# A 512-column product over both halves of the activations, and an earlier first up load, in a float32 transformer chain

## The chip, the core and the metric

The kernel runs on one core of one Trainium2 chip. The metric is the device time of the whole kernel in microseconds (us). Five engines work side by side: TensorE (PE) multiplies, its weight loads are listed as PEld; VectorE (DVE) and ScalarE (ACT) work element by element; GpSimd (POOL) does little here; SyncE (SP) issues the weight loads. Each engine takes its own instructions in a fixed order and waits on semaphores for the others.

## The reference, cut to what matters

Two models run one after the other; the change touches the first, `first_block`, alone. It has two layers, and in each layer two feed-forward networks of the same form, so four of them run in all.

```python
def swiglu(h, w_in, w_out):              # h 256 x 1024, w_in 1024 x 5632, w_out 2816 x 1024
    gate, up = jnp.split(h @ w_in, 2, axis=-1)
    return (jax.nn.silu(gate) * up) @ w_out

for l in range(DEPTH):                   # DEPTH = 2
    x = x + 0.5 * swiglu(rms_norm(x, ffn1_norm[l]), ffn1_w_in[l], ffn1_w_out[l])
    x = x + hybrid_mixer(rms_norm(x, mix_norm[l]), ...)
    x = x + 0.5 * swiglu(rms_norm(x, ffn2_norm[l]), ffn2_w_in[l], ffn2_w_out[l])
```

The second model (attention, a long convolution, a dense feed-forward network and a mixture of eight experts) follows and is left as it is.

## The kernel before, in words

**Two parts of each number.** Every float32 operand is split into a high part, which a fast product takes exactly, and the low rest. `split` does that: ACT copies the high part (L251), DVE subtracts it from the source (L252). A product of two such operands is then three products on PE, made by `mm3`: high by high (L290), high by low (L291), low by high (L292).

**Weights.** Weights are loaded 1 MB at a time by `load_raw` (L258) into one of three raw buffers (`wr_66`, `wr_67`, `B_72`) that are used in turn; SP issues these loads in one order. `cut` splits a raw buffer, 1024 columns at a time, into pair buffers (`wp_68` to `wp_71`, `B_73`, `B_74`), which are also used in turn. So the high copy waits until the load has landed and until PE has done with the weights that the pair buffer held before.

**The feed-forward network.** `ffn` walks over the 2816 inner columns in units of 512 (five full units and one of 256). A unit is up (two loads, `w_in`), the next unit's gate (two loads, `w_in`) and down (two loads, `w_out`). The first unit's gate and up are made the other way round, with the activations as PE's weights, and aren't touched by the change beyond the load. For every later unit the inner `gemm` makes a group of 128 inner columns by all 256 tokens with `gemm_feat`: 8 steps over the 1024 inputs, three products of 256 columns in each, 24 products in all, and two groups share one bank of PSUM. `Silu` (ACT, L414) or the multiplication of up by gate (DVE, L433) reads that bank whole, 512 columns at once.

**Banks.** `mmb` hands out the two banks of PSUM named `mm` in turn. PE may begin a new bank only when what was in it has been read.

**Activations.** `feat` lays out the split activations. For 1024 inputs by 256 tokens it makes one tile of high parts and one tile of low parts (`t_77`, `t_78`).

**Order.** A scheduler places the instructions of all engines when the program is built. Background work of the second model (its modulation vectors, L852 to L879, and its long filters, L949 to L1025) is strewn over these stages at low priority.

Of the kernel before, what the change touches and what calls it, by code (L numbers as in the profile page):

```python
# [20 lines left out]
P = 128  # L21
D = 1024
KD = D // P
S = 256
NB = S // P
DFF = 2816
# [91 lines left out]
class Feat:  # L118
# [3 lines left out]

    def span(self, k, n, s):
        c = slice(k % self.per, k % self.per + n)
        hi, lo = self.parts[k // self.per]
        return hi[:, c, s], lo[:, c, s]

    def at(self, k, s):
        hi, lo = self.parts[k // self.per]
        return hi[:, k % self.per, s], lo[:, k % self.per, s]  # L130


class Entry:
# [38 lines left out]
class K:  # L172
# [64 lines left out]
        return self.sb.tile([P, 2048], dt, tag=tag, name=self.nm(tag), bufs=self.BUFS[tag])  # L237

    def feat(self, kt, T):
        per = min(kt, 2048 // T)  # L240
        parts = []
        for _ in range(0, kt, per):
            if per * T <= 1024:
                t = self.tile([P, 2, per, T], "feat", dt=F32R)
                parts.append((t[:, 0], t[:, 1]))
            else:
                parts.append(tuple(self.tile([P, per, T], "feat", dt=F32R) for _ in range(2)))
        return Feat(parts, per)

    def split(self, hi, lo, src, eng=None):  # L250
# [51 lines left out]
    def gemm_feat(self, out, hT, wk, c0, s=slice(0, S)):  # L302
        kt = len(wk)
        c = slice(c0, c0 + P)
        for k in range(kt):
            wh, wl = wk[k]
            self.mm3(out, wh[:, c], wl[:, c], *hT.at(k, s), k == 0, k == kt - 1)

    def tok_steps(self, out, hT, b, wk):
        s = slice(b * P, (b + 1) * P)  # L310
# [67 lines left out]
    def ffn(self, jobs, nb=NB):  # L378
        nc = self.nc
        units = []  # L380
        for job in jobs:
            F = job["w"][0].shape[1]
            for f0 in range(0, F, 512):
                n = min(512, F - f0)
                units.append((job, f0, n, f0 + n == F))

        def gemm(hT, wk, n):
            if nb == 1:
                pg = self.mmb()[:, :n]
                self.gemm_tok(pg, hT, 0, wk)  # L390
                yield pg
                return
            T = nb * P
            for c0 in range(0, n, 2 * P):
                pg = self.mmb()
                for c in range(2):
                    self.gemm_feat(pg[:, c * T : (c + 1) * T], hT, wk, c0 + c * P)
                yield pg

        def gate(job, f0, n, last):  # L400
            if f0 == 0:
# [14 lines left out]
            return out  # L416

        def up(job, f0, n, last, parts):
            wk = job.pop("up", None) or self.load_wk(job["w"][1], f0, n)
            out = []  # L420
            if f0 == 0 and nb > 1:
                out = [self.tile([P, 2, 512], "gT", dt=F32R) for _ in range(n // S)]
# [64 lines left out]
        for i, u in enumerate(units):  # L487
            parts = up(*u, nxt)
# [13 lines left out]
            else:  # L502
                tail(*u[:3], held, parts, u[0]["next"]())

    def ffn_first(self, x, entry, w_in, w_out, nxt):
        nc = self.nc

        def end(b, dn):
            for h in range(2):
                c = slice(h * 512, (h + 1) * 512)  # L510
                nc.vector.scalar_tensor_tensor(
                    out=x[:, b, c], in0=dn[h], scalar=0.5, in1=x[:, b, c], op0=ALU.mult, op1=ALU.add
                )

        got = []

        def after():
            got.append(nxt and Entry(self, x, *nxt))
            return got[0]

        self.ffn([dict(w=(w_in[:, :DFF], w_in[:, DFF:], w_out), hT=entry.hT, first=entry.gemm(), end=end, next=after)])
        return got[0]

    def conv_glu(self, hT, w):
# [1209 lines left out]
def body(k, outs):  # L1734
# [13 lines left out]
    k.nr, k.nw = -1, -1  # L1748
    e.fetch()
    e.fetch()  # L1750
    load(1)
    e.rows(1)

# [4 lines left out]
        k.plan_filters()  # L1758
    for l in range(2):
        k.quota = QUOTAS[2 * l]  # L1760
        e = k.ffn_first(x, e, A["ffn1_w_in"][l], A["ffn1_w_out"][l], mix[l])
        e = k.mixer(x, l, e, ins["ffn2"][l])
        if l == 1:
            hT = k.feat(KD, 4 * P)
            k.plan_ctx(hT)
        k.quota = QUOTAS[2 * l + 1]
        e = k.ffn_first(x, e, A["ffn2_w_in"][l], A["ffn2_w_out"][l], None if l else ins["ffn1"][1])
# [50 lines left out]
```

## Time and profile before

| what | value |
|---|---|
| median of 3 runs | 2943.09 us (2939.08 to 2945.89) |
| profiled execution, its own time | 2937.49 us |
| span of its trace | 2935.8 us |
| PE busy | 2850.5 us (97%) |
| DVE busy | 2201.8 us (75%) |
| ACT busy | 1588.2 us (54%) |
| mean granted TensorE clock | 0.991 |

The profiled execution is one run, 5.6 us below the median of the timed runs. The span is the time from its first to its last instruction, 1.7 us less than its own time. Busy times are means over stages that are unlike each other; a stage has to be looked at by itself.

### The profile page before, as it was taken

How to read it: one execution, taken by the hardware profiler on the slowest of the kernel's cores; microseconds unless marked ns; L12 is line 12 of the kernel's file. 1: busy time of each engine (PE TensorE's matmuls, PEld its weight loads, DVE VectorE, ACT ScalarE, POOL GpSimd, SP SyncE). 2: the span in 40 equal slices, each digit the busy share in tenths (PEclk: the TensorE clock that was granted, in tenths of full speed). 3: DMA queues.
4: the chain of work that ended last, by engine and by line, in shares of the span. 5: the costliest groups of instructions: out<-in, count | busy, mean ns of one | idle time of the engine just before them, and what ended most of it. 6: DMA issues, size and time to landing. Idle time of an engine off the chain costs nothing. (4 is left out here: it accounts for less than half of the span.)

```text
span 2935.8 us, 40815 instructions
## 1 busy us (share of the span) xinstructions
PE 2850.5 (97%) x15778; PEld 2449.8 (83%) x15778; DVE 2201.8 (75%) x3391; ACT 1588.2 (54%) x2365; POOL 169.0 (6%) x249
## 2 busy tenths in 40 slices
PE   7999999999999998999999999999899999999997
PEld 6998789899878997888788888788788888888886
DVE  6778677777977756654458876666698999999997
ACT  5545654554475554432343323544487777777775
POOL 1000200100010000000000000100000000000000
PEclk9999999999999999999999999999999999999999
DMA  7654466656546643142334653335799999999995
GB/s 257 221 197 168 145 217 225 215 202 225 200 140 213 212 155 120 58 111 100 129 126 162 201 201 113 100 106 157 258 347 340 331 358 345 348 350 348 345 339 188
DMA packets 286922, 629.19 MB, mean 214 GB/s; under 512 B 12318, under 2 KB 59152, under 8 KB 286592
## 3 DMA queue, kind: packets, MB, share of 16 engines
q1 hardware_dynamic: 260160, 552.11, 54.0%
q0 software_dynamic: 26128, 73.93, 7.8%
q8 instruction: 126, 2.06, 0.3%
q14 instruction: 76, 0.62, 0.1%
q10 hardware_dynamic: 432, 0.46, 0.0%
HBM read 622.70 MB, written 3.75 MB: 213 GB/s over the span
## 5 line engine op out<-in xcount | busy, mean ns | idle before, releaser
L252 DVE TENSOR_TENSOR wp<-wr,wp 128x1024 fp32r<-128x1024 f32 (+3 forms) x449 | 528.0, 1189 | 167.8 <-ACT wp L251 161.4
L251 ACT ACTIVATE wp<-wr 128x1024 fp32r<-128x1024 f32 (+3 forms) x449 | 453.6, 1030 | 303.9 <-PE mm L292 83.0
L290 PE MATMUL mm<-t,wp 128*128 128x256 f32 (+1 forms) x1360 | 449.7, 331 | 0.4 <-ACT t L414 0.2
L292 PE MATMUL mm<-t,wp 128*128 128x256 f32 (+1 forms) x1360 | 425.4, 314 | 0.2 <-DVE wp L252 0.2
L291 PE MATMUL mm<-t,wp 128*128 128x256 f32 (+1 forms) x1360 | 424.5, 312 | 0.0
L252 DVE TENSOR_TENSOR B<-B,B 128x1024 fp32r<-128x1024 f32 x302 | 361.5, 1222 | 53.6 <-ACT B L251 50.9
L251 ACT ACTIVATE B<-B 128x1024 fp32r<-128x1024 f32 x302 | 312.8, 1055 | 121.1 <-PE acc L292 37.2
L290 PE MATMUL mm<-wp,t 128*128 128x512 f32 (+2 forms) x880 | 343.2, 392 | 5.7 <-ACT t L251 2.5
L291 PE MATMUL mm<-wp,t 128*128 128x512 f32 (+2 forms) x880 | 340.4, 387 | 4.2 <-DVE wp L252 4.1
L292 PE MATMUL mm<-wp,t 128*128 128x512 f32 (+2 forms) x880 | 339.2, 387 | 4.0 <-DVE t L252 4.0
L291 PE MATMUL acc<-wp,t 128*128 128x512 f32 (+2 forms) x760 | 289.8, 383 | 2.5 <-DVE wp L252 2.4
L290 PE MATMUL acc<-wp,t 128*128 128x512 f32 (+2 forms) x760 | 284.9, 386 | 4.3 <-ACT t L251 3.2
L292 PE MATMUL acc<-wp,t 128*128 128x512 f32 (+2 forms) x760 | 285.5, 383 | 1.4 <-DVE t L252 1.3
L290 PEld LDWEIGHTS mm<-t,wp 128*128 128x128 f32 x1360 | 259.6, 191 | 20.7 <-issue 8.2
L291 PEld LDWEIGHTS mm<-t,wp 128*128 128x128 f32 x1360 | 259.9, 191 | 19.1 <-issue 8.7
L252 DVE TENSOR_TENSOR wp<-B,wp 128x1024 fp32r<-128x1024 f32 x208 | 247.5, 1220 | 36.8 <-ACT wp L251 35.4
L292 PEld LDWEIGHTS mm<-t,wp 128*128 128x128 f32 x1360 | 259.1, 191 | 15.8 <-issue 1.0
L251 ACT ACTIVATE wp<-B 128x1024 fp32r<-128x1024 f32 x208 | 215.7, 1056 | 70.6 <-PE mm L292 37.2
L861 DVE SCALAR_TENSOR_TENSOR B<-B,cs,B 128x256 f32<-128x256 f32 x560 | 250.6, 480 | 3.7
L290 PEld LDWEIGHTS mm<-wp,t 128*128 128x128 f32 x880 | 167.5, 190 | 39.3 <-ACT t L251 4.4
L292 PEld LDWEIGHTS mm<-wp,t 128*128 128x128 f32 x880 | 167.4, 190 | 36.9 <-DVE t L252 6.1
L291 PEld LDWEIGHTS mm<-wp,t 128*128 128x128 f32 x880 | 167.5, 190 | 36.1 <-DVE wp L252 6.6
(378 smaller groups left out, 5388.0 us busy)
## 6 DMA issues: line engine op xcount, KB each, us to landing
B<-in_moe_w_gate_dram SPq DMA_DIRECT2D x65, 1024.0 KB, 7.2
B<-in_moe_w_up_dram SPq DMA_DIRECT2D x63, 1024.0 KB, 7.1
B<-in_moe_w_down_dram SPq DMA_DIRECT2D x62, 1024.0 KB, 6.8
wr<-in_ffn_w_in_dram SPq DMA_DIRECT2D x60, 1024.0 KB, 5.2
B<-in_w_mod_dram POOLq DMA_DIRECT2D x48, 1024.0 KB, 5.9
B<-in_ffn_w_in_dram SPq DMA_DIRECT2D x28, 1024.0 KB, 5.1
wr<-in_ffn_w_out_dram SPq DMA_DIRECT2D x28, 1024.0 KB, 4.9
wr<-in_w_in_dram SPq DMA_DIRECT2D x28, 1024.0 KB, 5.2
```

The costliest lines, as they stand in the source:

```text
L251: self.nc.scalar.activation(hi, src, AF.Copy)
L252: (eng or self.nc.vector).tensor_tensor(out=lo, in0=src, in1=hi.bitcast(F32), op=ALU.subtract)
L290: mm(out, lhsT=lh, rhs=rh, start=first, stop=False)
L291: mm(out, lhsT=lh, rhs=rl, start=False, stop=False)
L292: mm(out, lhsT=ll, rhs=rh, start=False, stop=last)
L861: nc.vector.scalar_tensor_tensor(out=acc, in0=raw[:, kk], scalar=cs[:, v, kk : kk + 1], in1=acc, op0=ALU.mult, op1=ALU.add)
```

## The change

In every feed-forward network of the first block, all units but the first: the high weights take the high and the low part of the activations as one moving operand of 512 columns (`gemm_two`), and the low weights take the high part alone into the second half of the same bank. A group of 128 inner columns now fills a bank by itself, with 8 products of 512 columns and 8 of 256. The two halves have to be added: ACT copies the second half into a new tile `sums`, DVE adds the first half, and `Silu` and the multiplication read `sums`. So that a step's high and low parts lie in one tile, `feat` makes two tiles of four steps each, with both parts in each. Apart from that, the first load of the first network's up weights is written directly behind the two loads of the gate, and `up` takes it over as `begun`.

```diff
     def feat(self, kt, T):
-        per = min(kt, 2048 // T)
+        per = min(kt, (1024 if T == S else 2048) // T)
         parts = []
         for _ in range(0, kt, per):
             if per * T <= 1024:
                 t = self.tile([P, 2, per, T], "feat", dt=F32R)
-                parts.append((t[:, 0], t[:, 1]))
+                parts.append((t[:, 0], t[:, 1], t))
...
+    def both(self, k):
+        return self.parts[k // self.per][2][:, :, k % self.per]
...
+    def gemm_two(self, out, hT, wk, c0):
+        mm = self.nc.tensor.matmul
+        c = slice(c0, c0 + P)
+        kw = dict(skip_group_check=True)
+        for k in range(len(wk)):
+            wh, wl = wk[k]
+            x = hT.both(k)
+            mm(out, lhsT=wh[:, c], rhs=x, start=k == 0, stop=k == len(wk) - 1, **kw)
+            mm(out[:, S:], lhsT=wl[:, c], rhs=x[:, 0], start=False, stop=k == len(wk) - 1, **kw)
...
             for c0 in range(0, n, 2 * P):
-                pg = self.mmb()
+                sums = self.tile([P, 512], "sums")
                 for c in range(2):
-                    self.gemm_feat(pg[:, c * T : (c + 1) * T], hT, wk, c0 + c * P)
-                yield pg
+                    pg = self.mmb()
+                    self.gemm_two(pg, hT, wk, c0 + c * P)
+                    part = sums[:, c * S : (c + 1) * S]
+                    nc.scalar.activation(part, pg[:, S:], AF.Copy)
+                    nc.vector.tensor_tensor(out=part, in0=part, in1=pg[:, :S], op=ALU.add)
+                yield sums
...
         def up(job, f0, n, last, parts):
-            wk = job.pop("up", None) or self.load_wk(job["w"][1], f0, n)
+            begun = job.pop("begun", None)
+            if begun:
+                rest = job["w"][1].rearrange("(k p) n -> p k n", p=P)[:, 4:, f0 : f0 + n]
+                wk = self.cut(*begun) + self.load_w(rest)
+            else:
+                wk = job.pop("up", None) or self.load_wk(job["w"][1], f0, n)
...
     e.fetch()
     e.fetch()
+    up = k.load_raw(A["ffn1_w_in"][0].rearrange("(k p) n -> p k n", p=P)[:, :4, DFF : DFF + 512])
     load(1)
```

The scheduler's order differs from before in the four feed-forward stages and the stretches that border on them (there in background work and its loads), and in a branch at the end of the program (a second pass over the experts, for more than 128 tokens of one expert); elsewhere it is the same. At three places it shows what moves.

**On PE, the second unit's gate.** `mm_846` and `mm_807` are a bank of PSUM, `wp` and `B` weights, `t_77` and `t_78` activations. Before, two steps over the inputs and the start of the third:

```order
L290 MATMUL mm_846<-t_77,wp_70 128x256 [waits DVE_49]
L291 MATMUL mm_846<-t_78,wp_70 128x256
L292 MATMUL mm_846<-t_77,wp_70 128x256
L290 MATMUL mm_846<-t_77,wp_70 128x256
L291 MATMUL mm_846<-t_78,wp_70 128x256
L292 MATMUL mm_846<-t_77,wp_70 128x256
L290 MATMUL mm_846<-t_77,wp_71 128x256
```

Now, the same steps:

```order
L319 MATMUL mm_807<-t_77,wp_70 128x512 [waits DVE_49]
L320 MATMUL mm_807<-t_77,wp_70 128x256
L319 MATMUL mm_807<-t_77,wp_70 128x512
L320 MATMUL mm_807<-t_77,wp_70 128x256
L319 MATMUL mm_807<-t_77,wp_71 128x512
```

Three products of 256 columns have become one of 512 and one of 256; the columns in all are the same.

**On SP, the start of the program.** Before, with `in_ffn_w_in` the gate's and then the up weights:

```order
L1738 DMA x<-in_x_dram 128x1024
L258 DMA wr_66<-in_ffn_w_in_dram 128x4x512
L258 DMA wr_67<-in_ffn_w_in_dram 128x4x512
L1738 DMA x<-in_x_dram 128x1024
L258 DMA wr_66<-in_ffn_w_in_dram 128x4x512 [waits DMAHW2_49,DVE_49]
L258 DMA wr_67<-in_ffn_w_in_dram 128x4x512 [waits DMAHW4_49,DMAHW0_49,DVE_49]
L258 DMA B_72<-in_ffn_w_in_dram 128x4x512 [waits DMAHW1_49]
```

Now:

```order
L1761 DMA x<-in_x_dram 128x1024
L261 DMA wr_66<-in_ffn_w_in_dram 128x4x512
L261 DMA wr_67<-in_ffn_w_in_dram 128x4x512
L1761 DMA x<-in_x_dram 128x1024
L261 DMA B_72<-in_ffn_w_in_dram 128x4x512
L261 DMA wr_66<-in_ffn_w_in_dram 128x4x512 [waits DMAHW2_49,DMAHW0_49,DVE_49]
L261 DMA wr_67<-in_ffn_w_in_dram 128x4x512 [waits DMAHW4_49,DMAHW1_49,DVE_49]
```

The load into `B_72`, the first half of the first up weights, stood seventh, behind two loads that wait for their buffers to be cut; it now stands fifth and waits for nothing.

**On ACT, a unit in the middle of the second network of layer 0.** Rows of L251 (L254 now) are the high copies of weights, `t_4039` is a `sums` tile, `bg` rows are background work. Before:

```order
L414 ACTIVATE t_4249<-mm_4200 128x512 [waits PE_49]
L251 ACTIVATE wp_70<-wr_67 128x1024 [waits DMAHW7_49,PE_49,Activation_49]
L251 ACTIVATE wp_71<-wr_67 128x1024 [waits PE_49,Activation_49]
L251 ACTIVATE B_73<-B_72 128x1024 [waits DMAHW0_49,DVE_49,PE_49]
L251 ACTIVATE B_74<-B_72 128x1024 [waits DVE_49,PE_49]
L876 ACTIVATE B_149,mod_142<-bg_3681 128x128 [waits PE_49]
L876 ACTIVATE B_149,mod_142<-bg_3681 128x128
L960 ACTIVATE B_149<-B_149 64x256 [waits DVE_49]
L876 ACTIVATE B_149,mod_141<-bg_3687 128x128 [waits PE_49]
L876 ACTIVATE B_149,mod_141<-bg_3687 128x128
L251 ACTIVATE t_4369<-t_4198 128x512 [waits DVE_49]
```

Now:

```order
L430 ACTIVATE t_3969<-t_3930 128x512 [waits DVE_49]
L899 ACTIVATE B_150,mod_143<-bg_3461 128x128 [waits PE_49]
L899 ACTIVATE B_150,mod_143<-bg_3461 128x128
L254 ACTIVATE B_73<-B_72 128x1024 [waits DMAHW1_49,Activation_49]
L254 ACTIVATE B_74<-B_72 128x1024 [waits Activation_49]
L983 ACTIVATE B_150<-B_150 64x256 [waits DVE_49]
L412 ACTIVATE t_4039<-mm_4040 128x256 [waits PE_49]
L899 ACTIVATE B_150,mod_142<-bg_3467 128x128 [waits PE_49]
L899 ACTIVATE B_150,mod_142<-bg_3467 128x128
L412 ACTIVATE t_4039<-mm_4059 128x256 [waits PE_49]
L1030 ACTIVATE B_152<-B_152 128x256 [waits DVE_49]
L412 ACTIVATE t_4082<-mm_4083 128x256 [waits PE_49]
```

Each bank of up is now emptied by an ACT copy of its own (L412), and the first of them stands behind the high copies of the next gate's first load (`B_73`, `B_74` from `B_72`); before, no bank of up was emptied by ACT.

## Rows read from the trace of the kernel before

**Rows 1.** The page: span, and part 1, busy time by engine.

```profile
span 2935.8 us, 40815 instructions
## 1 busy us (share of the span) xinstructions
PE 2850.5 (97%) x15778; PEld 2449.8 (83%) x15778; DVE 2201.8 (75%) x3391; ACT 1588.2 (54%) x2365; POOL 169.0 (6%) x249
```

**Rows 2.** Windows: busy time in the four feed-forward stages.

```profile
core 0: us, PE busy (x) PEld busy (x) DVE busy (x) ACT busy (x) POOL busy (x), PEclk, DMA share, GB/s
37.00:214.00 177.00, 177.00 (x1210) 162.22 (x1209) 128.28 (x224) 87.74 (x133) 13.89 (x19) 1.00 0.65 221
370.00:545.00 175.00, 173.72 (x1200) 160.06 (x1198) 129.14 (x229) 85.33 (x140) 14.45 (x19) 1.00 0.66 225
565.00:748.00 183.00, 183.00 (x1252) 169.14 (x1251) 129.35 (x216) 89.36 (x146) 14.71 (x20) 1.00 0.64 215
898.00:1075.00 177.00, 176.18 (x1206) 163.43 (x1206) 123.83 (x200) 85.30 (x139) 9.32 (x14) 1.00 0.60 207
```

**Rows 3.** Timeline of PE: products of 256 columns (start, duration, operation).

```profile
49.73 0.28 PE L291 MATMUL mm<-t,wp 128*128 128x256 f32 x1
...
54.77 0.28 PE L291 MATMUL mm<-t,wp 128*128 128x256 f32 x1
```

**Rows 4.** Timeline of PE: from 256 columns to 512 columns.

```profile
58.06 0.28 PE L292 MATMUL mm<-t,B 128*128 128x256 f32 x1
58.18 0.40 PE L290 MATMUL acc<-wp,t 128*128 128x512 f32 x1
...
62.74 0.39 PE L291 MATMUL acc<-wp,t 128*128 128x512 f32 x1
```

**Rows 5.** Timeline of PE: from 512 columns to 256 columns.

```profile
69.65 0.39 PE L292 MATMUL acc<-wp,t 128*128 128x512 f32 x1
69.88 0.28 PE L290 MATMUL mm<-t,B 128*128 128x256 f32 x1
69.99 0.28 PE L291 MATMUL mm<-t,B 128*128 128x256 f32 x1
70.11 0.28 PE L292 MATMUL mm<-t,B 128*128 128x256 f32 x1
```

**Rows 6.** Timeline of the start: ACT's wait, and PE around it.

```profile
25.63 1.06 ACT L251 ACTIVATE wp<-wr 128x1024 fp32r<-128x1024 f32 x1 [1.50 <-PE mm L292]
...
29.29 0.39 PE L292 MATMUL mm<-wp,t 128*128 128x512 f32 x1
...
30.82 2.00 ACT L251 ACTIVATE B<-B 128x1024 fp32r<-128x1024 f32 x2 [4.12 <-DMA B<-in_ffn_w_in_dram]
...
31.93 0.50 PE L290 MATMUL mm<-B,t 128*128 128x512 f32 x1 [2.25 <-ACT B L251]
...
33.19 0.70 PE L291 MATMUL mm<-B,t 128*128 128x512 f32 x1 [0.76 <-DVE B L252]
...
33.69 0.63 PE L292 MATMUL mm<-B,t 128*128 128x512 f32 x1
...
36.67 0.42 PE L290 MATMUL mm<-B,t 128*128 128x512 f32 x1
```

**Rows 7.** Timeline of SP: the issues at the start.

```profile
1.25 0.98 SPq L258 DMA_DIRECT2D wr<-in_ffn_w_in_dram  x2
2.27 0.84 SPq L1738 DMA_DIRECT2D x<-in_x_dram  x1
15.83 2.64 SPq L258 DMA_DIRECT2D wr<-in_ffn_w_in_dram  x2
18.52 0.50 SPq L258 DMA_DIRECT2D B<-in_ffn_w_in_dram  x1
```

**Rows 8.** Groups by line and shape: count, busy us, mean ns, idle before.

```profile
L252 DVE TENSOR_TENSOR wp<-wr,wp 128x1024 fp32r<-128x1024 f32 x413 | 499.0, 1221 | 158.7 <-ACT wp L251 155.4
L251 ACT ACTIVATE wp<-wr 128x1024 fp32r<-128x1024 f32 x413 | 428.0, 1055 | 286.1 <-PE mm L292 83.0 <-PE acc L292 72.1 <-PE mm L291 68.2
L251 ACT ACTIVATE t<-t 128x512 fp32r<-128x512 f32 x128 | 79.5, 628 | 157.3 <-DVE t L1492 72.0 <-DVE t L433 57.6 <-DVE t L1341 14.5
L414 ACT ACTIVATE t<-mm 128x512 f32<-128x512 f32 x84 | 49.5, 593 | 69.2 <-PE mm L292 69.0
L251 ACT ACTIVATE t<-tr 128x256 fp32r<-128x256 f32 x31 | 11.7, 379 | 18.1 <-DVE t L252 7.0 <-PE tr L1252 5.8 <-PE tr L438 3.0
L1000 DVE TENSOR_TENSOR B<-B,bg 128x256 f32<-128x256 f32 x16 | 6.7, 416 | 3.0 <-PE bg L999 2.0 <-ACT B L997 1.0
```

**Rows 9.** The page, part 6: weight loads, KB each, us to landing.

```profile
wr<-in_ffn_w_in_dram SPq DMA_DIRECT2D x60, 1024.0 KB, 5.2
B<-in_ffn_w_in_dram SPq DMA_DIRECT2D x28, 1024.0 KB, 5.1
```

**Rows 10.** Timeline of PE: two background products among those of 256 columns.

```profile
57.01 0.28 PE L291 MATMUL mm<-t,B 128*128 128x256 f32 x1
57.12 0.27 PE L873 MATMUL bg<-mats,B 128*128 128x128 f32 x1
57.15 0.36 PE L292 MATMUL mm<-t,B 128*128 128x256 f32 x1
57.35 0.27 PE L873 MATMUL bg<-mats,B 128*128 128x128 f32 x1
57.38 0.36 PE L290 MATMUL mm<-t,B 128*128 128x256 f32 x1
57.58 0.28 PE L291 MATMUL mm<-t,B 128*128 128x256 f32 x1
```

More of the change, by code (lines that the diff above doesn't have):

```diff
@@ L124, in span @@
         c = slice(k % self.per, k % self.per + n)
-        hi, lo = self.parts[k // self.per]
+        hi, lo, _ = self.parts[k // self.per]
         return hi[:, c, s], lo[:, c, s]
     def at(self, k, s):
-        hi, lo = self.parts[k // self.per]
+        hi, lo, _ = self.parts[k // self.per]
         return hi[:, k % self.per, s], lo[:, k % self.per, s]
+    def both(self, k):
+        return self.parts[k // self.per][2][:, :, k % self.per]
 class Entry:
@@ L244, in feat @@
                 t = self.tile([P, 2, per, T], "feat", dt=F32R)
-                parts.append((t[:, 0], t[:, 1]))
+                parts.append((t[:, 0], t[:, 1], t))
             else:
-                parts.append(tuple(self.tile([P, per, T], "feat", dt=F32R) for _ in range(2)))
+                parts.append((*(self.tile([P, per, T], "feat", dt=F32R) for _ in range(2)), None))
         return Feat(parts, per)
@@ L392, in gemm @@
                 return
-            T = nb * P
             for c0 in range(0, n, 2 * P):
-                pg = self.mmb()
+                sums = self.tile([P, 512], "sums")
                 for c in range(2):
-                    self.gemm_feat(pg[:, c * T : (c + 1) * T], hT, wk, c0 + c * P)
-                yield pg
+                    pg = self.mmb()
[4 more added lines that the diff above has]
+                yield sums
         def gate(job, f0, n, last):
@@ L503, in ffn, with ffn_first @@
                 tail(*u[:3], held, parts, u[0]["next"]())
-    def ffn_first(self, x, entry, w_in, w_out, nxt):
+    def ffn_first(self, x, entry, w_in, w_out, nxt, up=None):
         nc = self.nc
@@ L519, in after @@
             return got[0]
-        self.ffn([dict(w=(w_in[:, :DFF], w_in[:, DFF:], w_out), hT=entry.hT, first=entry.gemm(), end=end, next=after)])
+        job = dict(w=(w_in[:, :DFF], w_in[:, DFF:], w_out), hT=entry.hT, first=entry.gemm(), end=end, next=after)
+        job["begun"] = up
+        self.ffn([job])
         return got[0]
@@ L1760, in body @@
         k.quota = QUOTAS[2 * l]
-        e = k.ffn_first(x, e, A["ffn1_w_in"][l], A["ffn1_w_out"][l], mix[l])
+        e = k.ffn_first(x, e, A["ffn1_w_in"][l], A["ffn1_w_out"][l], mix[l], None if l else up)
         e = k.mixer(x, l, e, ins["ffn2"][l])
```

## The prediction

> **What bounds the kernel now.** I read the page first: PE is busy for 2850.5 of 2935.8 us, DVE for 75% and ACT for 54% [rows 1]. Such shares are means over unlike stages, so the second view is the windows of the four stages that the change touches. There PE is busy for 177.00 of 177.00, 173.72 of 175.00, 183.00 of 183.00 and 176.18 of 177.00 us, at a granted clock of 1.00, with DVE at 70 to 74% and ACT near half [rows 2]. So in these stages PE never waits for anyone: what shortens PE's own row of work shortens the kernel, and any new wait of PE lengthens it. The third view is PE's timeline, where the distance from start to start tells what a product costs (the durations overlap and tell nothing). Products of 256 columns start 0.120 us apart: 42 steps from 49.73 to 54.77 [rows 3]. Products of 512 start 0.228 apart: 20 steps from 58.18 to 62.74 [rows 4]. So each has a part of about 0.013 us that does not grow with the columns (twice 0.120 less 0.228 is 0.012). The fourth view is the start. ACT waits 4.12 us there for the load of the first up weights, PE stands for 2.25 and 0.76 us behind it, and then runs at half pace for some 3 us [rows 6].
>
> **The change part by part.**
>
> *Fewer products.* A full unit has four groups of 128 inner columns for gate and four for up, the last unit two and two. A network has four full units after the first and the small one, so 18 groups for gate and 18 for up. Each group loses one product in each of 8 steps: 4 x 36 x 8 = 1152 products fewer, with the same columns. A step cost 3 x 0.120 = 0.360 us. It now costs a product of 512 and one of 256 in turn. If each keeps its own distance, that is 0.228 + 0.120 = 0.348, a gain of 0.012. Where the two sizes meet in the trace, the 512 is followed after 0.227 (69.65 to 69.88, read with the rounding of the row) and that first 256 by its successor after 0.11 instead of 0.12 [rows 5], which makes 0.340 and a gain of 0.020. From 256 to 512 the distance is 0.12 again [rows 4]. In the new order every 256 stands behind a 512, as in rows 5, but before a 512, as in rows 4. I take the middle, 0.016: 1152 x 0.016 = **18.4 us less**, with bounds of 13.8 and 23.0.
>
> A rule of the Trainium skill speaks for less: "TensorE: Matmul & The Clock Gate", section "Back-to-back issue gap", gives columns through 2.4 GHz plus some 2.5 ns for each product. By that a dropped product would save 2.5 ns, 2.9 us in all; the rows show distances 11 to 12 ns longer than it gives (0.120 and 0.228 against 0.109 and 0.216), so I keep to the rows.
>
> *The first up load.* The load into `B_72` was issued at 18.52, behind two loads at 15.83 that wait for their buffers, and was waited for until 30.82; now it goes out right behind the loads of 1.25 to 2.27 [rows 7]. From PE's last product before the wait (29.29) to 36.67 there are ten steps [rows 6], which at 0.228 take 2.28 us instead of 7.38. **5.1 us less**, if nothing else is late. In the new order the products on the first half of these weights are even drawn into the gate's, and the second half is cut while they run, so I take it whole; its bounds are 0 and 5.1.
>
> *Copies and additions.* There are 144 ACT copies from PSUM and 144 DVE additions, 36 of each in a stage. The nearest rows are 0.379 us for an ACT copy of 128x256 from PSUM and 0.416 for a DVE addition of 128x256 with one input in PSUM [rows 8]. A stage thus gets 13.6 us of ACT and 15.0 of DVE. In the first window DVE goes from 128.3 to 143.3 of some 171 us, 84%, and ACT to 101.3, 59%: both still have room beside PE, and I cost them at nothing in themselves. `Silu` from SBUF instead of PSUM adds some 0.035 us (0.628 against 0.593 for such rows [rows 8]) under the same cover. Without cover, copy and addition together would cost 144 x 0.80 = 114 us.
>
> *The new wait.* A bank of `mm` was filled in 48 x 0.120 = 5.8 us and read by one instruction; it is now filled in 8 x 0.344 = 2.75 us, and PE may come back to it only when a copy and then an addition have run. So the cover is one other bank, 2.75 us, and whatever products of down the scheduler put between. The bare chain of 0.38 + 0.42 fits; the question is what stands ahead of the copy in ACT's fixed order. The tightest place that I find is that shown on ACT: the copy of up's first bank stands behind the high copies of a load into `B_72`. I walk it with these rows, as an estimate, from the start of the last bank of gate. PE lets go of the first old pair after a quarter of that bank, 0.7. ACT's two high copies of the old `B_72` (1.06 each) end at 1.8 and 2.8, DVE's two subtractions (1.22) at 3.0 and 4.2 [rows 8], and the buffer is free. The load lands 5.1 later [rows 9], at 9.3. Its two high copies end at 10.4 and 11.4, the bank's copy at 11.8, DVE's second subtraction at 12.6 and the addition at 13.0. PE wants the bank after the rest of gate (2.75), 24 products of down (24 x 0.228 = 5.5), two banks of up (5.5) and four background products (0.10 each: 57.01 to 57.58 is 0.57 for three products of 0.120 and two of these [rows 10]): 14.1. So 1.1 us are left, once in each of the 20 units. Loads that share the queues with background traffic are later than 5.1; the one of 18.52 took 12.3 [rows 6, 7]. I put the waits that this makes at 0.1 us a unit, **2 us more**; bounds are 0 and what the slower rival gives.
>
> *The sum*: -18.4 - 5.1 + 2.0 = -21.5 us. Against the profiled execution's own 2937.5 us that is 2916.0. The median of the runs shown is 2943.1, 5.6 above it; the time that I give is on that footing, **2921.6 us**, a change of -0.73%.
>
> **The rivals.**
>
> *ACT's order holds the banks back (slower).* If the weight loads come later than in the walk, the high copies that wait for them hold the copies of banks queued behind them on ACT, the additions behind those on DVE, and PE stands before a bank. Everything beyond 1.1 us of lateness is paid by PE, in each of 20 units. It decides from 23.5 / 20 = 1.2 us of wait a unit. A landing after 8.2 us instead of 5.1 makes 2 us a unit, 40 in all: 2943.1 - 23.5 + 40 = 2960. For it speaks that the order also puts a down load (`w_out`) ahead of the next gate's in SP's queue. Against it: DVE and ACT have room, the loads' median is 5.1 to 5.2 us [rows 9], and the same scheduler's order left no wait in 177 us [rows 2]. Chance 0.13, half of it only enough to eat the gain.
>
> *A 512-column product in two pieces costs as two.* The high and low halves of its moving operand lie 4 KB apart. No row shows such a product. If each piece pays the fixed part, a step costs 0.36 as before and the first term is nothing: 2943.1 - 5.1 + 2 = 2940. Chance 0.06. Beside it, the Trainium skill's "PSUM — Partial Sum Buffer", section "Specifications (TRN2)", says that a non-contiguous access pattern slows products markedly; the product's output, of which that page speaks, is one run here, and no run here shows the other.
>
> *The fixed part isn't a product's.* If the 0.012 belongs to the columns' own stream or to weight loads in some way that a mix doesn't save, and only some 2.5 ns are saved with each product, 1152 x 0.0025 = 2.9 us: 2943.1 - 2.9 - 5.1 + 2 = 2937. Chance 0.06, the size that the rule above gives.
>
> *The start stays as long.* The wait goes, but the second half of the up weights or the next gate comes late in its place: 2943.1 - 18.4 + 2 = 2926.7. Against it: that half's load was issued at 15.83 in the trace and ACT's copy of it at 25.63 waited for PE, not for the load [rows 6, 7]. Chance 0.10.
>
> **How the numbers follow.** The forecast has 0.65, the start's rival 0.10, the two rivals on the products 0.12, the slow one 0.13. The forecast's own bounds are 2943.1 - 28.1 = 2915 and 2943.1 - 13.8 - 5.1 + 6 = 2930. To leave no more than 2 in 10 outside, the range reaches up over the products' rivals, to 2940, and down to 2914. A difference under 0.2%, 5.9 us, is about what a measurement of this kernel can't tell from none. Faster by more takes the forecast, the start's rival and a third of the products' rivals: 0.79. Within it: the rest of these and half of the slow rival, 0.14. Slower: 0.07.
>
> **What would show it.** PE's timeline in these stages should show a 512 and a 256 in turn, 0.34 to 0.35 us a step. PE's busy time should fall by about the sum, with its window still full. The wait of 2.25 us at 31.9 should be gone. Waits of PE for DVE's addition (`sums`) should be rare and under a microsecond. I am wrong if the windows show PE idle before the first product of a bank, with ACT waiting for a weight load ahead of a copy, or if a step costs 0.36.

## The result and the profile after

The changed kernel is slower: median 2984.9 us (2984.2 to 2988.9, five runs) against 2940.7 us for the kernel before (2938.1 to 2945.9), a ratio of 1.0143 [1.0131, 1.0155]. The forecast was 2921.6 us, and its range ended at 2940.

The page of the changed kernel, span and busy times (against [rows 1]):

```profile
span 2983.2 us, 38785 instructions
PE 2861.0 (96%) x14626; PEld 2396.5 (80%) x14626; DVE 2252.9 (76%) x3535; ACT 1631.5 (55%) x2509; POOL 169.0 (6%) x249
```

The 1152 products are gone (15778 less 14626), yet PE is busy longer. Windows of the four networks, changed kernel (against [rows 2]):

```profile
37.00:217.00 180.00, 173.32 (x905) 144.33 (x904) 139.31 (x259) 97.91 (x171) 14.72 (x20) 0.98 0.63 211
370.00:558.00 188.00, 178.04 (x920) 148.01 (x919) 148.43 (x279) 98.00 (x180) 14.47 (x20) 0.98 0.63 216
575.00:770.00 195.00, 187.61 (x982) 157.25 (x981) 146.84 (x267) 102.99 (x192) 15.25 (x21) 0.99 0.62 211
920.00:1122.00 202.00, 182.17 (x913) 152.61 (x912) 136.96 (x234) 97.35 (x175) 9.37 (x14) 0.93 0.53 180
```

PE now stands for 6.7, 10.0, 7.4 and 19.8 us (window less PE's busy time), where it stood for 0 to 1.3, and its granted clock is no longer 1.00. DVE is busy for 68 to 79% and ACT for about half: neither is full. From the last update of `x` on, the rest of the program takes 1850.2 us as against 1850.1, so the whole loss lies ahead of it.

PE's waits in these stretches and the mixers between them, changed kernel from 37 to 1133 (us in total, times, longest; two rows at the mixers, at the mark, and the smaller rows are left out):

```profile
PE mm L319 <- DVE t L413: 12.5, 10, 2.9
PE acc L293 <- ACT t L254: 9.7, 4, 4.1
...
PE bg L1033 <- DVE B L1032: 4.1, 2, 3.9
PE bg L1046 <- DVE B L1039: 3.9, 2, 3.6
PE bg L896 <- DVE B L884: 3.9, 1, 3.9
PE tr L369 <- DVE t L1064: 3.4, 2, 3.2
PE tr L369 <- ACT t L1081: 3.2, 2, 1.6
```

L413 is the new addition: PE waits for it before a bank only ten times, 12.5 us in all. More, 18.5 us in the rows shown, goes to products of the background (`bg`, and `tr` for the context rows), and 4.1 once to down's first product behind the last bank.

**A bank held back**, in the second network, changed kernel (timeline: start, us):

```profile
437.09 0.37 SPq L261 DMA_DIRECT2D B<-in_ffn_w_in_dram  x1
444.73 2.01 ACT L254 ACTIVATE B<-B 128x1024 fp32r<-128x1024 f32 x2 [4.40 <-DMA B<-in_ffn_w_in_dram]
446.16 0.28 PE L320 MATMUL mm<-t,wp 128*128 128x256 f32 x1
446.65 0.64 ACT L412 ACTIVATE t<-mm 128x256 f32<-128x256 f32 x2
446.97 0.88 DVE L884 SCALAR_TENSOR_TENSOR B<-B,cs,B 128x256 f32<-128x256 f32 x2
447.76 1.22 DVE L255 TENSOR_TENSOR B<-B,B 128x1024 fp32r<-128x1024 f32 x1
448.90 0.42 DVE L413 TENSOR_TENSOR t<-t,mm 128x256 f32<-128x256 f32 x1
449.37 0.50 PE L319 MATMUL mm<-t,wp 128*128 128x512 f32 x1 [2.93 <-DVE t L413]
450.62 0.63 PE L319 MATMUL mm<-t,wp 128*128 128x512 f32 x1
451.26 0.63 PE L319 MATMUL mm<-t,wp 128*128 128x512 f32 x1
```

The load comes 7.5 us after its issue, ACT stands behind it with the bank's copies, and DVE's addition stands behind background work (L884) and a subtraction (L255). The last two rows show a second price: steps of 0.64 us instead of 0.35 a microsecond after PE has begun again. The Trainium skill ("Perfetto Trace Analysis", section "Tensor Engine Instruction (MATMUL, LD_WEIGHTS)") says that ACT and DVE take their work strictly first in, first out; these rows agree, since the addition's inputs were there at 447.29 (446.65 and 0.64) and it began at 448.90.

**The start**, changed kernel, PE's timeline (against [rows 6]): 11 steps in 2.50 us, without a wait.

```profile
29.36 0.39 PE L295 MATMUL mm<-wp,t 128*128 128x512 f32 x1
...
31.86 0.39 PE L294 MATMUL mm<-wp,t 128*128 128x512 f32 x1
```

**The step**, changed kernel, PE's timeline (against [rows 3]): 0.23 and 0.12 in turn, 14 steps from 440.97 to 445.92, 0.354 each; over 931 steps of all four networks that meet no wait and no half clock the mean is 0.350.

```profile
440.97 0.40 PE L319 MATMUL mm<-t,wp 128*128 128x512 f32 x1
441.20 0.28 PE L320 MATMUL mm<-t,wp 128*128 128x256 f32 x1
...
445.92 0.40 PE L319 MATMUL mm<-t,wp 128*128 128x512 f32 x1
```

### The profile page after: what moved, and what is told of

It reads as the page before. It is cut to its first block, busy times and chain, and to the rows that moved or that the text cites. A ratio compares the mean times of both kernels' runs of the same rounds, so it can differ in the third digit from the quotient of the medians.

```text
span 2983.2 us, 38785 instructions
## 1 busy us (share of the span) xinstructions
PE 2861.0 (96%) x14626; PEld 2396.5 (80%) x14626; DVE 2252.9 (76%) x3535; ACT 1631.5 (55%) x2509; POOL 169.0 (6%) x249
## 5 line engine op out<-in xcount | busy, mean ns | idle before, releaser
L255 DVE TENSOR_TENSOR wp<-wr,wp 128x1024 fp32r<-128x1024 f32 (+3 forms) x449 | 526.3, 1188 | 154.1 <-ACT wp L254 147.9
L254 ACT ACTIVATE wp<-wr 128x1024 fp32r<-128x1024 f32 (+3 forms) x449 | 450.8, 1029 | 261.6 <-PE mm L295 79.9
L255 DVE TENSOR_TENSOR B<-B,B 128x1024 fp32r<-128x1024 f32 x302 | 359.9, 1219 | 60.7 <-ACT B L254 58.6
L254 ACT ACTIVATE B<-B 128x1024 fp32r<-128x1024 f32 x302 | 311.3, 1054 | 111.0 <-DMA B<-in_ffn_w_in_dram 30.8
L319 PE MATMUL mm<-t,wp 128*128 128x512 f32 x784 | 289.7, 405 | 9.5 <-DVE t L413 9.5
L255 DVE TENSOR_TENSOR wp<-B,wp 128x1024 fp32r<-128x1024 f32 x208 | 247.4, 1218 | 35.4 <-ACT wp L254 34.1
L884 DVE SCALAR_TENSOR_TENSOR B<-B,cs,B 128x256 f32<-128x256 f32 x560 | 250.9, 479 | 4.0
L254 ACT ACTIVATE wp<-B 128x1024 fp32r<-128x1024 f32 x208 | 215.7, 1055 | 68.6 <-PE mm L295 35.5
L293 PE MATMUL mm<-t,wp 128*128 128x512 f32 (+1 forms) x576 | 225.8, 392 | 0.6 <-DVE t L1515 0.6
L320 PE MATMUL mm<-t,wp 128*128 128x256 f32 x784 | 223.7, 286 | 0.0
L295 PE MATMUL mm<-t,wp 128*128 128x512 f32 (+1 forms) x576 | 201.0, 351 | 0.2 <-DVE wp L255 0.2
L294 PE MATMUL mm<-t,wp 128*128 128x512 f32 (+1 forms) x576 | 201.0, 349 | 0.0
L319 PEld LDWEIGHTS mm<-t,wp 128*128 128x128 f32 x784 | 149.8, 191 | 46.5 <-DVE t L413 7.3
```

Source lines behind the costliest of these rows:

```text
L254: self.nc.scalar.activation(hi, src, AF.Copy)
L255: (eng or self.nc.vector).tensor_tensor(out=lo, in0=src, in1=hi.bitcast(F32), op=ALU.subtract)
L293: mm(out, lhsT=lh, rhs=rh, start=first, stop=False)
L294: mm(out, lhsT=lh, rhs=rl, start=False, stop=False)
L295: mm(out, lhsT=ll, rhs=rh, start=False, stop=last)
L319: mm(out, lhsT=wh[:, c], rhs=x, start=k == 0, stop=k == len(wk) - 1, **kw)
```

## The experiments

Three theories stood at the beginning. **A**: SP's new order, with a down load ahead of the next gate's, makes the gate's weights late, and all else follows. **B**: the copy and the addition are late in the fixed queues of ACT and DVE whatever the loads' order. **C**: the merged product itself costs. **D** came later: it takes the background work in the same queues to make them late. Each ratio is to the kernel before on the same chip; "early load alone" is the base, as both kernels of a pair have it.

| run | ratio to before [95%] | median, us |
|---|---|---|
| e1 early load alone | 0.9975 [0.9963, 0.9986] | 2937.4 |
| e2 half of each bank read, no sum | 1.0017 [1.0007, 1.0027] | 2949.9 |
| e3 SP held in program order | 1.0668 [1.0650, 1.0686] | 3140.5 |
| e4 one reduction | 1.0094 [1.0077, 1.0111] | 2974.1 |
| e5 loads chained | 1.0161 [1.0141, 1.0180] | 2989.5 |
| e6 products split again | 1.0155 [1.0138, 1.0172] | 2991.8 |
| e7 three banks | 1.0135 [1.0118, 1.0152] | 2984.3 |
| e8 all three cures | 1.0071 [1.0053, 1.0088] | 2963.8 |
| e9 early load, background behind | 1.1151 [1.1132, 1.1169] | 3281.8 |
| e10 changed, background behind | 1.1207 [1.1188, 1.1225] | 3295.7 |
| e11 half read, background behind | 1.1116 [1.1097, 1.1134] | 3271.8 |
| e12 one reduction, background behind | 1.1156 [1.1137, 1.1175] | 3282.8 |
| e13 changed, old last unit, background behind | 1.1123 [1.1104, 1.1141] | 3274.8 |
| e14 changed, old last unit | 1.0086 [1.0069, 1.0103] | 2967.8 |
| e15 the same, one reduction, background spread | 1.0038 [1.0024, 1.0052] | 2955.4 |
| e16 early load, background spread | 0.9982 [0.9972, 0.9992] | 2938.8 |
| e17 e14 without network 4's background | 1.0242 [1.0223, 1.0260] | 3015.8 |
| e18 early load without network 4's background | 1.0227 [1.0209, 1.0245] | 3011.7 |

**e1, the early load alone.** The kernel before with the last piece of the front's diff and `begun`, nothing else.

> The kernel before with the early first up load alone. The term of the prediction is 5.1 us less, so 2935.6 against the 2940.7 of the kernel before; the rival (the start stays as long) gives 2940.7. All theories of the loss agree here, since none of them touches this part: if it comes out above 2945, the early load itself spoils the order and is part of the loss.

Measured 0.25% less, 7.0 us between the medians. The start's term was right within that, and it is the only part of the change that pays as it stands.

**e2, no sum.**

```diff
-                sums = self.tile([P, 512], "sums")
...
+                pgs = [self.mmb() for _ in range(2)]
+                for c, pg in enumerate(pgs):
                     self.gemm_two(pg, hT, wk, c0 + c * P)
...
+                yield pgs
...
```

`Silu` and the multiplication read the first half of each bank and the second is never read.

> The changed kernel without the copies and the additions: Silu and the multiplication read the first half of each bank straight from PSUM, as two instructions of 256 columns. It leaves out the sum of the two halves (the cross terms of gate and up are computed and never read). Theory A (the order of SP's loads) and theory B (the copy and the addition stand in fixed queues behind work that waits for loads, and PE waits for the bank) both expect the waits gone: 1152 products fewer at the 0.010 us of the profile after are 11.5 us, the start 5.1, so about 2924. Theory C (the products themselves lose, by the clock or by the mix of sizes) expects it to stay above 2940.

Neither: 35 us less than the changed kernel (2949.9 against 2984.9), but 12.5 more than the early load alone. The sum is most of the loss and not all of it.

**e3 and e5, the order of SP's loads.** e3 holds all of SP's instructions in program order; e5 only ties each weight load behind the one before:

```diff
+        with self.tc.issue_after(self.held) if self.held else nullcontext():
+            d = self.nc.sync.dma_start(out=raw[:, : a * b].rearrange("p (a b) -> p a b", a=a), in_=src)
+        if self.held:
+            self.held = d.ins
```

> The changed kernel with the weight loads of a network held in the order in which the program writes them, as before the change: a down load no longer stands in front of the next gate's. Theory A (the load order delays the gate's weights, and all else follows) expects most of the 36 us of PE's waits gone, with the half-clock stretches behind them: 2925 to 2945. Theory B (the bank's copy and addition are late in ACT's and DVE's queues whatever the load order) expects little: 2970 to 2990.

> The changed kernel, each weight load of a network issued after the one that the program writes before it; SP's other instructions stay free, unlike in the run with SP's whole order held. The order of weight loads is then that of the kernel before. Theory A (a down load ahead of the next gate's makes the gate's late, and all else follows) expects most of PE's 36 us of waits gone: 2930 to 2950. Theory B (copy and addition stand in fixed queues behind cuts of weights, whatever the load order) expects 2970 to 2990.

e3 doesn't tell: SP also issues the stores of the background's filters, which e3 pins in program order too, and in its trace PE waits for background in the first network already (e3, PE's timeline):

```profile
83.44 1.22 PE L1025 MATMUL bg<-B,B 64*128 64x256 f32 x2 [4.25 <-ACT B L986]
```

e5 is the clean form. It has the load order of before and is no faster than the changed kernel (1.0161 against 1.0143): **theory A falls**.

**e4 and e7, the bank's chain.** e4 sums a bank by one DVE instruction, e7 gives gate and up a third bank.

```diff
-                    nc.scalar.activation(part, pg[:, S:], AF.Copy)
-                    nc.vector.tensor_tensor(out=part, in0=part, in1=pg[:, :S], op=ALU.add)
+                    nc.vector.tensor_reduce(out=part, in_=pg.rearrange("p (j s) -> p s j", j=2), op=ALU.add, axis=AX.X)
```

```diff
-                    pg = self.mmb()
+                    pg = self.bank(("mm", "mm", "tr")[self.turns % 3])
+                    self.turns += 1
```

> The changed kernel with the two halves of a bank summed by one DVE reduction over a view of the bank, in place of ACT's copy and DVE's addition. ACT, where the copies of late loads stand, is then out of the bank's chain. Theory B with ACT's queue as the place expects about two thirds of the loss gone, 2935 to 2955. Theory B with DVE's queue as the place expects little, 2965 to 2985, since the subtractions of late weights stand in front of the reduction just as they stood in front of the addition. Theory A expects no change, 2980, as the order of loads stays nearly the same (a down load ahead of the gate's in 4 of the first network's units).

> The changed kernel with a third bank in the rotation of gate and up: the one that transposes use is borrowed for every third group of 128 inner columns. PE then comes back to a bank after two others, 5.6 us instead of 2.8. Theory B expects the waits on a bank (2 to 3 us each in the profile after) mostly gone, and those of background products for late background operands left: 2950 to 2970. Theory A expects the late gate weights to stop PE all the same, 2975 to 2990.

e4 gives back 11 us (14 by the ratios), a quarter to a third of the loss: what theory B expected with DVE's queue as the place, and less than with ACT's. e7 gives back nothing, with 5.6 us of cover for a bank instead of 2.8. In its trace the waits for a bank's sum are down from 12.5 to 2.6 us, but up to the last update of `x` PE stands for 57.2 us as against 57.8. The third bank is taken from the transposes, and other waits have come in their place (3.1 us of products before the borrowed bank, and 6.0 before the context rows' transposes instead of 3.4). So relieving the bank alone doesn't help; e7 can't tell whether these waits were cheap or only moved.

**e6, the products of before in the new banks.** The high product is made twice with 256 columns, into each half of the bank; each half is opened by a start flag of its own. The sum that e6 leaves is another one; it has the copies and additions of the changed kernel, and only its time is used.

> The changed kernel with the products of before: the high weights take the two parts of the activations in two products of 256 columns, one into each half of the bank, and copies, additions, layout and early load stay as changed. If the merged product is a gain of 0.010 us in each of 1152 steps, and the loss is all from the way the banks are emptied, this is 11 us slower than the changed kernel, 2996. If the loss came from PE going through a bank faster than copy and addition can follow (theory B in its form of cover: 2.8 us a bank), the slower products give 0.08 us more a bank and nothing else changes. If the merged product itself costs (theory C), this is faster than 2985.

2991.8 is 7 us above the changed kernel, where 11 were expected; the intervals of the two ratios overlap, so e6 alone doesn't show a gain of the merged product. Theory C would have it below 2985: **theory C falls**.

**e8, all three cures together** (e4, e5 and e7).

> The changed kernel with the weight loads chained in the order of before, the third bank, and one DVE reduction in place of copy and addition. If nothing but these waits makes the loss, it should come near the sum of the prediction with the product's gain as measured: 2943 - 11.5 - 6 = 2925. If it stays above 2943, some of the loss lies elsewhere (the smaller groups by which the banks change hands, DVE's added time, background work).

Still 0.71% above before. Some of the loss was elsewhere, and the lengths of the networks (from the last update of `x` ahead of one to the last in it; the first from 37 us) showed where: with the cures the first and second networks were shorter than with the early load alone (182.2 and 205.7 us against 184.7 and 213.2), the fourth was 20 us longer (215.7 against 195.9). The two mixers were longer too, by 7.0 and 6.6 us (130.0 and 135.2 against 123.0 and 128.6); that was not followed up.

**e9 to e12, without background in the networks.** The tasks are drained in one piece behind the last network.

```diff
-            self.bg(self.quota[i % 6])
+            self.bg(0)
...
+    k.late = 0
+    k.bg(10000)
```

> The kernel before with the early load, and the background work of the four networks taken out of them and drained in one piece behind the last one (nothing is left out, it only stands elsewhere). It is the base for the three runs beside it, which drain the same work at the same place. Expected longer than the kernel before by some 50 to 150 us, all of it behind the fourth network; the networks themselves shorter by their background products, without waits of PE.

> The changed kernel with the background work drained behind the last network. Theory D (the copies and additions are late because ACT's and DVE's fixed queues also hold background work, and because background products in PE's fixed order wait for their own late operands) expects it faster than the run with the early load alone and no background by 1152 x 0.010 = 11 us or a little less. Theory B (copy and addition are late behind cuts of weights, with or without background) expects it slower than that run by 20 to 50 us. The load order with a down load in front of the gate's stays as in the changed kernel, so theory A too expects it slower.

> The kernel that reads half of each bank, with the background drained behind the last network; it leaves out the sum of the halves. It tells what the merged product alone is worth where nothing disturbs: 11 us less than the early load alone without background, if 0.010 us a step is all there is; no less, if the smaller groups by which banks change hands cost as much.

> One DVE reduction in place of copy and addition, with the background drained behind the last network. Theory D expects about the time of the changed kernel without background, within 5 us, since both then have room; theory B with ACT as the place expects it 10 us or more faster than that.

The base went up by 339 us, far more than expected; only differences within the four count. Without background the changed kernel loses 14 us to the base instead of 48, e12 loses 1, and e11 gains 10. By the traces, up to the last update of `x`, it is 16.0 and 4.6 lost and 8.1 gained (ends at 1038.7, 1027.3 and 1014.6 against e9's 1022.7). So e10 meets neither theory: D expected it 11 us below the base, B 20 to 50 above. The first network of e9 and of e11 (windows; PE is never idle in either):

```profile
37.00:210.00 173.00, 173.00 (x1178) 160.89 (x1177) 91.34 (x94) 77.08 (x89) 1.23 (x3) 1.00 0.55 190
```

```profile
37.00:208.00 171.00, 171.00 (x890) 145.43 (x889) 91.96 (x103) 77.64 (x98) 1.24 (x3) 1.00 0.55 192
```

It is 2 us shorter, as are the other three: that is what 288 products fewer in a network are worth, 7 ns each. And ACT waits for weight loads in e11 as it does in the changed kernel (ACT's waits from 37 to 208), at no cost at all:

```profile
ACT wp L254 <- DMA wr<-in_ffn_w_in_dram: 21.7, 6, 4.0
```

In e11 no bank's copy stands behind these loads. In e13 (below) copies do, and the first network is as short as e11's (e13, ACT's waits and the window):

```profile
ACT wp L254 <- DMA wr<-in_ffn_w_in_dram: 18.0, 6, 4.3
```

```profile
37.00:208.00 171.00, 170.98 (x918) 146.33 (x917) 103.30 (x126) 86.42 (x120) 1.24 (x3) 1.00 0.56 191
```

So late loads on ACT don't cost by themselves. What e10 still loses stands at one place in each network, its end (timeline of e10; the same wait of 4.07 stands at 512.54, 707.27 and 1024.09):

```profile
191.51 0.28 PE L320 MATMUL mm<-t,B 128*128 128x256 f32 x1
191.77 1.06 ACT L254 ACTIVATE B<-B 128x1024 fp32r<-128x1024 f32 x1 [0.36 <-PE mm L319]
192.74 0.36 ACT L412 ACTIVATE t<-mm 128x256 f32<-128x256 f32 x1
192.86 1.23 DVE L255 TENSOR_TENSOR B<-B,B 128x1024 fp32r<-128x1024 f32 x1 [0.19 <-ACT B L254]
194.00 0.41 DVE L413 TENSOR_TENSOR t<-t,mm 128x256 f32<-128x256 f32 x1
194.45 0.69 DVE L454 TENSOR_TENSOR t<-t,t 128x512 f32<-128x512 f32 x1
195.18 0.63 ACT L254 ACTIVATE t<-t 128x512 fp32r<-128x512 f32 x1 [2.08 <-DVE t L454]
195.86 0.80 PE L293 MATMUL acc<-B,t 128*128 128x512 f32 x1 [4.07 <-ACT t L254]
```

Down needs the last group of up, and between its last product and down there are now, one after the other, a high copy of weights, the bank's copy, a subtraction of weights, the addition, the multiplication and the split. With the one reduction of e12 the wait there is 1.4 us in each network. In the changed kernel itself background products stand in this gap in the first three networks (PE waits 3.6 us at 211.90, 3.9 at 554.22, 1.7 and 1.8 from 763.04 on), and down in the fourth (4.07 at 1118.12).

**e13 and e14, the last unit in the old form** (two groups in a bank, read whole), without background and with it.

```diff
+            if n < 512:
+                pg = self.mmb()
+                for c in range(2):
+                    self.gemm_feat(pg[:, c * S : (c + 1) * S], hT, wk, c * P)
+                yield pg
+                return
```

> The changed kernel without background in the networks, and the last unit of each network (256 columns) in the form of before: two groups share a bank, read whole, no copy and no addition. If the wait of 4.07 us at the end of each network is the whole price of emptying the banks where nothing disturbs, four such waits with the slow stretch behind each, 17 to 22 us, are gone: 3274 to 3279, that is 3 to 8 us less than the early load alone without background. If the copies and additions cost all along the network, it stays above 3285.

> The same last unit in the old form, in the changed kernel with its background where it was. If the prices add up, 17 to 22 us less than the changed kernel, 2963 to 2968. If the background's order decides, anything from 2950 to 2990.

e13 is 21 us below e10 and 7 below the base (3.5 by the traces, 1019.2 against 1022.7): without background the end of the networks was the whole price, and the copies and additions of all other units are hidden, but for 3 to 5 us at most (e13 against e11, which has none: 3.0 between the medians, 4.6 by the traces). Of theory B this leaves the end of the networks. e14 is 17 us below the changed kernel, as expected from adding up.

**e15 and e16, background spread evenly** over the units.

```diff
-QUOTAS = [(4, 3, 2, 0, 0, 0), (4, 3, 3, 1, 0, 0), (4, 3, 2, 0, 0, 0), (4, 4, 2, 0, 0, 0)]
+QUOTAS = [(2, 2, 2, 2, 1, 0), (3, 3, 2, 2, 1, 0), (2, 2, 2, 2, 1, 0), (2, 2, 2, 2, 2, 0)]
```

> The last unit in the old form, one DVE reduction in place of copy and addition, and the background tasks of each network spread over five units (2, 2, 2, 2, 1) in place of (4, 3, 2). Theory D in its form of crowding expects the loss nearly gone: 2925 to 2940, below the kernel before. If spreading does nothing, the two other edits give about 2944 less 0 to 5 against the run with one reduction (2974 - 17 = 2957).

> The kernel before with the early load and the same spreading, without merged products: the base for the run beside it. Its networks hardly wait, so spreading can give at most the 10 us of waits that they have: 2930 to 2940.

e15 comes out at 2955.4, where adding up the two other edits gave 2957: crowding in the first units is not it. (Theory D in that form had expected 2925 to 2940.)

**e17 and e18, network 4's background taken out alone.** By the lengths of the networks and mixers, 20 of the 28.7 us between the traces of e14 and of the early load alone (2964.6 and 2935.9) lie in the fourth network (216.0 against 195.9).

> The changed kernel with the last units in the old form and the ten background tasks of the fourth network (modulation vectors, context rows) drained behind it; those of the other three networks stay. Theory D in this place: the fourth network is at most 2 us longer than in the run beside it (it was 20 us longer with its background), and the whole kernel within 12 us of that run. If the late copies and additions are a matter of the merged form alone, the difference stays near 30 us.

> The early load alone, with the background tasks of the fourth network drained behind it: the base for the run beside it. Longer than the kernel before by 20 to 100 us, all of it behind the fourth network.

The difference falls from 1.11% (e14 less e1) to 0.15%. The fourth network of e1 and of e14 (with background), then of e18 and of e17 (without):

```profile
890.00:1086.00 196.00, 193.04 (x1283) 176.97 (x1282) 134.21 (x215) 92.56 (x150) 11.32 (x17) 1.00 0.59 200
```

```profile
898.00:1114.00 216.00, 199.00 (x1026) 168.02 (x1025) 146.20 (x247) 103.30 (x182) 11.39 (x17) 0.94 0.53 180
```

```profile
886.00:1074.00 188.00, 186.00 (x1234) 171.33 (x1232) 96.38 (x101) 80.58 (x95) 1.72 (x3) 1.00 0.50 171
```

```profile
898.00:1086.00 188.00, 185.37 (x980) 158.02 (x978) 108.87 (x134) 90.78 (x127) 1.72 (x3) 1.00 0.51 173
```

With this background the merged form is 20 us longer: PE stands for 17 us instead of 3, and is busy for 6 more at a granted clock of 0.94. Without it, the two are alike (187.4 and 188.0 by their lengths). Theory D holds there. How it comes about can be read in the changed kernel (timeline):

```profile
1028.20 2.01 ACT L254 ACTIVATE B<-B 128x1024 fp32r<-128x1024 f32 x2 [4.30 <-DMA B<-in_ffn_w_in_dram]
1029.30 2.36 DVE L255 TENSOR_TENSOR B<-B,B 128x1024 fp32r<-128x1024 f32 x2 [4.67 <-ACT B L254]
1032.95 0.66 PE L369 MATMUL tr<-mats,t 128*128 128x128 f32 x4 [3.19 <-DVE t L1064]
1035.21 1.12 PE L369 MATMUL tr<-mats,t 128*128 128x128 f32 x4 [1.59 <-ACT t L1081]
1038.29 0.77 PE L319 MATMUL mm<-t,wp 128*128 128x512 f32 x1 [1.97 <-DVE t L413]
```

ACT waits for a load, the context rows' norm stands behind it on ACT and DVE, and PE has the transposes of these rows in its fixed order, ahead of gate's next bank: three waits, 6.8 us. Some 45 us earlier it goes the same way, with products of the modulation in front (waits of 3.9, 1.2, 1.6 and 2.0). That the context rows rather than the modulation's products beside them carry most of the 20 us is read from these waits and was not tried by itself.

## Why the prediction was wrong

The loss against before, put together from differences of ratios (1% is 29.4 us; the first row is known to some 3 us, a difference of two ratios to 6 to 8, one of four to some 10):

| part | from | us |
|---|---|---|
| early load | e1 | -7 |
| products, less copies and additions of full units, without background | e13 - e9 | -8 |
| end of the four networks | changed - e14 | +17 |
| network 4's background | (e14 - e1) - (e17 - e18) | +28 |
| background of networks 1 to 3 | (e17 - e18) - (e13 - e9) | +13 |
| sum (before rounding) | changed | +42 |

The sum comes out by construction, since each run but the changed kernel stands once with plus and once with minus. Two rows hold more than their names say. Behind the last update of `x` the instructions are the same in e17 and e18, yet they take 1925.5 and 1934.0 us, and in e13 and e9 2254.3 and 2260.2. In e18 PE's granted clock is lower there at one place (0.89 against 0.96 in 45 us, 116 us behind that update); more isn't known. By the lengths up to that update the fourth network's background is worth 20.7 us ((216.0 - 195.9) - (187.4 - 188.0)) and the products less copies and additions 3.5.

- **The bound.** That PE's row sets the time, and that any new wait lengthens it, was right. That DVE and ACT "both still have room" was right as a share (at most 79% and 54% in the windows above) and no guard: what counted was what stood ahead of one instruction.
- **Fewer products: right in sign, too large.** I took 0.016 us a step from a switch seen once [rows 5]. The step is 0.350 to 0.354, a gain of 0.006 to 0.010, and the runs give 8 (e11 and e9, the four networks' lengths) to 10 us (their medians) for all instead of 18.4, below the bound of 13.8. A 256 between two 512s does not start its successor any sooner than one among its like (0.12 after it in both). The Trainium skill's rule ("TensorE: Matmul & The Clock Gate", "Back-to-back issue gap"), which the page gives for a product by itself, has 2.5 ns a product, an estimate of 2.9 us in all. It is too small here: 8 to 10 us over 1152 products are 7 to 9 ns each.
- **The first up load: right,** 7.0 us against 5.1.
- **Copies and additions at nothing: right in the full units.** They last 0.373 and 0.413 us, close to the 0.379 and 0.416 of [rows 8], and without background cost 3 to 5 us in all.
- **The new wait: the step that failed.** I gave it 2 us, and it is 58 by the ratios, 17 + 28 + 13, and 50 by the lengths of the traces (46.7 from the early load alone to the changed kernel, and the 3.5 that the products give back). I walked one place, the copy of up's first bank behind a gate load, and called it the tightest. That place does fail as the slower rival says, when the load takes 7.5 us instead of 5.1, and the sign of being wrong that I had named (a wait before a bank, with a load ahead of its copy) was there, but such waits on a bank are 12.5 us in the whole trace. What I did not walk is the end of the network, where no products of down are left as cover: in e10, twelve of them stand at 186.07 to 188.59, ahead of the last bank, and none behind it. Nor did I ask which background products stand in PE's own order, although [rows 10] show two of them: PE waits for these as it does for a bank. And I gave no price to the slower steps behind each wait.
- **The rivals.** "ACT's order holds the banks back" had the sign and half the mechanism, with the wrong place: neither the load order (e5) nor the bank's cover (e7) moves the time. The two rivals on products would have been too small by themselves; the start did not stay long.

Open: the 13 us in networks 1 to 3 were not taken apart further. Three waits on banks behind late loads there (2.16 at 72.43, 2.93 at 449.37, 1.93 at 738.00) are a part, and the slow stretch behind the second; behind the two others PE goes on at full pace. With an uncertainty of some 10 us this row says little more than that something is left.

No version with merged products beat the kernel before; the early load alone does (0.9975), and it beats the changed kernel by 1.7%.

## What to carry to other kernels

When a change puts one more instruction between a product and its reader, walk the chain at every place where the reader has no other work in front of it, the last unit of a loop first, and not only at the busiest place. List what stands in PE's own order for other purposes: background products turn a late queue on ACT or DVE into a wait of PE. Here four ends of a network cost 17 us, and all the products saved gave back 8 to 10.

## What the runs showed of the hardware

A wait of PE can cost more than itself. Changed kernel, behind the wait of 4.07 at the end of the fourth network, and behind one of 2.16 at 72.43 (windows):

```profile
1117.50:1122.00 4.50, 3.88 (x9) 3.06 (x10) 0.69 (x1) 0.57 (x1) 0.00 (x0) 0.50 0.56 172
72.40:76.00 3.60, 3.57 (x20) 3.10 (x21) 3.60 (x10) 0.43 (x2) 0.00 (x0) 1.00 0.70 279
```

In the first PE is granted 0.50, the lower of its two levels (1.2 of 2.4 GHz): nine products take 0.43 us each where they take 0.228 at the other level [rows 4], 1.8 us on top of the 4.07. From 1122 to 1128 the clock is 0.93, and 1.00 behind that. In the second the clock stays at 1.00, so not every wait brings this about.

What it comes to over the networks and mixers can be read from two windows, the early load alone and the changed kernel, each up to its last update of `x`:

```profile
37.00:1086.30 1049.30, 1026.23 (x6616) 919.75 (x6615) 770.11 (x1329) 555.56 (x884) 99.20 (x145) 0.99 0.59 196
```

```profile
37.00:1133.00 1096.00, 1038.25 (x5469) 868.96 (x5468) 821.94 (x1475) 599.90 (x1028) 99.04 (x145) 0.97 0.55 187
```

The changed kernel is 46.7 us longer. For 34.7 of them PE stands (57.8 us instead of 23.1), and for 12.0 it is busier, although the products saved should make it 8 to 10 us less busy. So some 20 us, an estimate from these numbers, are the slower steps at the lower clock (0.97 against 0.99).
